# A chunked delta-rule recurrence: its output product in two PSUM banks, plain transposes of the keys, one prefix sum per pair of heads

## The chip, the cores and the metric

One NeuronCore of a Trainium2 chip runs the whole program in one launch. The metric is the device time of that launch in microseconds. Three runs of the kernel before are known, and one execution was profiled; every row below is from that one.

## The reference, cut to what matters

Two layers run over 1024 tokens of width 1024: a gated linear recurrence with convolution first, an RWKV-7 time mixer second, each followed by a SwiGLU and a gated projection. The change touches the RWKV-7 scan alone, which for each of 16 heads keeps a 64x64 state:

```
def step(S, inp):
    r_t, w_t, k_t, v_t, a_t, b_t = inp
    sa = jnp.einsum('bhvk,bhk->bhv', S, a_t)
    S = S * w_t[:, :, None, :] + sa[..., None] * b_t[:, :, None, :] + v_t[..., None] * k_t[:, :, None, :]
    y = jnp.einsum('bhvk,bhk->bhv', S, r_t)
    return S, y
```

The rest of the layer (projections, norms, SwiGLU, about 11,000 dense matmuls of 128x128 by 128x512) is the bulk of the arithmetic.

## The kernel before

Tokens are split into two halves of 512 (`t` = 0, 1), each half into eight chunks of 64. The scan is done chunk by chunk, for all 16 heads at once, two heads to a tile of 128 partitions (`HV` names the two halves E and O). It is cut into four streams, written as Python generators in `scan`:

- `stage1`, once per pair of heads and half, prepares: prefix sums of the log decay (`L`), the scaled keys `BK`, the products `sc` (masked into `ZL` and `AB`) and the transposed keys `bkt`, which go to DRAM as `bk`. The transposed keys are multiplied by the decay of the whole chunk, since the right operand of the product is `dg`, an identity whose rows POOL has scaled by `PC`.
- `inverse`, once per two pairs, inverts a triangular matrix per chunk and head in blocks (`w`, `n`, `u`, `w`, `v`).
- `stage2`, the recurrence, 16 steps in all (8 chunks, twice). Each step does three products into the one bank `zu`: z (from state `SV` and `ZL`), u (from `V` and z), and the state's increment (from `BKc` and `SU`); each waits for the copy of the one before it. DVE then adds the increment to `ss`, the state times the decay, worked out before. At the end of the step comes the output `y`: for each of 8 pairs and 2 heads one matmul over all 128 rows (state times `ZL`) and one over 64 rows (`SU` times `ZL`) that adds to it in the same 64x64 piece of the bank `y`.
- `norm2` normalizes the output of a half, two pairs at a time (`bsum`, `yv`), once all its steps are done.

The dense layers around it call `tick()` after every matmul. `tick` steps each stream whose wait has run out on a planner's clock (`self.clock`, advanced by an assumed time for each matmul) and, for streams that say so, once one or two PSUM banks of the ring `b` are taken to be free (`bank_free`, `BANKS`). PE's instructions stand in exactly this order: scan pieces between dense matmuls. `until` stops the dense work until a stream has reached a point. The scan's own PSUM is `zu`, `y` and `BANKS` banks `b`; the dense matmuls have three more (`mm`). The other engines' orders are the scheduler's: `ahead(n)` raises the priority of what stands under it.

Dense weights arrive as 128x512 pieces (`raw`, by SP's queue), are split by ACT (L239) and POOL (L240) into two parts `whl`, and are used by 12 matmuls each.

Of the kernel before, what the change touches and what calls it, by code (L numbers as in the profile page):

```python
# [8 lines left out]
F32 = mybir.dt.float32  # L9
F32R = mybir.dt.float32r  # L10
AF = mybir.ActivationFunctionType
ALU = mybir.AluOpType
# [3 lines left out]
TH = 512  # L16
# [8 lines left out]

BANKS = 3
PACE = ((3, 1200), (2.5, 200))
LEAD_O, LEAD_F, LEAD_E, LEAD_P = 2, 2, 1, 2  # L30
IN = 2
# [28 lines left out]
class Kern:  # L60
# [47 lines left out]
    def ahead(self, n):  # L108

        return self.tc.high_priority(n) if self.region else nullcontext()  # L110
# [811 lines left out]
    def scan_begin(self, sp, pp):  # L922
        nc, A = self.nc, self.A
        self.sp, self.spp = sp, pp
        self.zu = pp.tile([128, KD, 64], F32, name="zu")
        self.yp = pp.tile([128, KD, 64], F32, name="y")
        self.Pp = sp.tile([128, NC, 65], F32, name="Pp")
        nc.vector.memset(self.Pp[:, :, 0:1], 1.0)
        self.D16 = sp.tile([128, 32, 16], F32, name="D16")
        nc.vector.memset(self.D16, 0.0)  # L930
        self.O64 = sp.tile([128, 2 * NC, 64], F32, name="O64")
        nc.gpsimd.memset(self.O64, 0.0)

        self.zl_d = [self.dr.tile([128, NC, KD, 320], F32, name=f"zl{t}") for t in range(2)]
        self.bk_d = [self.dr.tile([128, NC, KD, 128], F32, name=f"bk{t}") for t in range(2)]
        self.inv_d = [self.dr.tile([128, NC, KD, 64], F32, name=f"inv{t}") for t in range(2)]
        self.y_d = [self.dr.tile([128, KD, TH], F32, name=f"y{t}") for t in range(2)]

    def scan(self):
# [45 lines left out]
        def c3(x):  # L985
            return x.rearrange("p (c s) -> p c s", s=64)
# [8 lines left out]
        def stage1():  # L995
            Pp = self.Pp

            def prep(t, j):
                at = ld("a", j, t)
                sw = ld("w", j, t)  # L1000
                kt = ld("k", j, t)
                L = tt("L")
                for c in range(0, TH, 64):
                    nc.vector.tensor_tensor_scan(
                        L[:, c : c + 64], self.ones[:, 0:64], sw[:, c : c + 64], 0.0, ALU.mult, ALU.add)
                nc.scalar.activation(Pp[:, :, 1:65], c3(L), AF.Exp, scale=-C0)
                nc.scalar.activation(L, L, AF.Exp, scale=C0)
                return at, kt, L, ld("q", j, t), sw

            nxt = None  # L1010
            for P, (t, g, jj) in enumerate(order):
# [17 lines left out]
                    PCs[t] = sp.tile([128, NC, KD], F32, tag="PC", name="PC", bufs=2)  # L1029
                PC = PCs[t][:, :, j]  # L1030
                nc.vector.tensor_copy(PC, Pp[:, :, 64])

                dg = sp.tile([128, NC, 64], F32, tag="dg", name="dg", bufs=1)
                nc.gpsimd.tensor_mul(dg, ident.unsqueeze(1).to_broadcast([128, NC, 64]), PC.unsqueeze(2).to_broadcast([128, NC, 64]))

                old = (P - 3) // 2
                yield 4000, False, (lambda: old < 0 or inv[old] >= 2)
# [49 lines left out]
                pss = [c3(big("bkt", e)) for e in (500, 900)]  # L1087
                for c in range(NC):
                    for hh, me, ot in HV:
                        self.mm(pss[hh][:, c, :], BK[me, c, :, :].rearrange("p i s -> p (i s)"), dg[me, c, :])  # L1090
                        self.clock -= 77
                evac()
                evac()
                with self.ahead(AHEAD_S1):
# [86 lines left out]
        def stage2():  # L1181
# [3 lines left out]
            def state():  # L1185
                return sp.tile([128, 2, KD, 64], F32, tag="SV", name="SV", bufs=2)
# [21 lines left out]
            for t in range(2):  # L1208
                yield 0, False, (lambda: inv[4 * t + 3] == 3 and s1[4 * t + 3] == 22 and all(have("v", j, t)() for j in range(KD)))
                PC = PCs[t]  # L1210
                nxt = load(t, 0, SV)
                yield C0LAT, False, None
                for c in range(NC):
                    ZL, V, SV = nxt
                    SU, BKc = load_u(t, c)
                    upd = not (t == 1 and c == NC - 1)
                    ps, yp = self.zu, self.yp
                    z = sp.tile([128, KD, 64], F32, tag="z", name="z", bufs=1)
                    at = self.clock
                    for j in range(KD):  # L1220
                        for hh, me, ot in HV:
                            self.mm(ps[me, j, :], ZL[:, j, hh * 128 : hh * 128 + 64], SV[:, hh, j, :])
                    self.clock = at + 650
                    with ahead():
                        nc.scalar.copy(z, ps)
                        if upd:
                            ss = sp.tile([128, KD, 64], F32, tag="ss", name="ss", bufs=1)
                            for hh, me, ot in HV:
                                nc.vector.tensor_mul(ss[me], SV[me, hh], PC[me, c, :].unsqueeze(2).to_broadcast([64, KD, 64]))
                            SVn = state()  # L1230
                        if c < NC - 1:
                            nxt = load(t, c + 1, SVn)
                    yield ZLAT, False, None
                    at = self.clock
                    for j in range(KD):
                        for hh, me, ot in HV:
                            self.mm(ps[me, j, :], V[me, j, :], z[me, j, :])
                    self.clock = at + 600
                    with ahead():
                        nc.scalar.copy(SU[E, 0], ps[E])  # L1240
                        nc.vector.tensor_copy(SU[O, 1], ps[O])
                    yield ULAT, False, None
                    at = self.clock
                    if upd:
                        for j in range(KD):
                            for hh, me, ot in HV:
                                self.mm(ps[me, j, :], BKc[:, j, hh * 64 : hh * 64 + 64], SU[:, hh, j, :])
                        with ahead():
                            for hh, me, ot in HV:
                                nc.vector.tensor_add(SVn[me, hh], ps[me], ss[me])  # L1250
                    for j in range(KD):
                        for hh, me, ot in HV:
                            self.mm(yp[me, j, :], SV[:, hh, j, :], ZL[:, j, hh * 128 + 64 : hh * 128 + 128], True, False)
                            self.mm(yp[me, j, :], SU[me, hh, j, :], ZL[me, j, 256:320], False, True)
                    self.clock = at + 2000
                    if c % 2 == 0:
                        ys = sp.tile([128, KD, 2, 64], F32, tag="yc", name="yc", bufs=1)
                    with ahead():
                        nc.scalar.copy(ys[:, :, c % 2, :], yp)
                    if c % 2:  # L1260
                        nc.sync.dma_start(self.y_d[t][:, :, c * 64 - 64 : c * 64 + 64], ys.rearrange("p j c k -> p j (c k)"))
                    if upd:
                        SV = SVn
                    s2[t] = c + 1
                    yield SLAT, False, None
# [223 lines left out]
```

## Time and profile before

| | us |
|---|---|
| median of 3 runs (lowest, highest) | 3225.04 (3216.24, 3226.09) |
| profiled execution, its own time | 3224.65 |
| its span, first to last instruction | 3222.9 |
| PE (matmul) busy | 3038.5, 94% |
| DVE, ACT, POOL busy | 50%, 42%, 40% |
| mean granted clock of TensorE | 0.950 of 2.4 GHz |

Busy shares are means over the whole span; which engine limits a stretch is read in the windows of that stretch. A matmul of plain fp32 leaves two records in the trace, so a block of 16 of them is a row of 32. The recurrence runs from about 1523 to 1766 us and from 2311 to 2535 us.

### The profile page before, as it was taken

The numbers are of one execution on the slowest core, as the hardware profiler recorded it, in microseconds if no ns is written. First come the engines' busy times: TensorE is split into PE (matmuls) and PEld (weight loads), VectorE is DVE, ScalarE is ACT, GpSimd is POOL, SyncE is SP. The second block draws the span as 40 slices with busy tenths as digits, with TensorE's granted clock in tenths as the row PEclk, the third lists the DMA queues.
The fourth block names the chain that finished last, engine by engine and source line by source line (L and its number), as shares of the span: only waits on it lengthen the run. The fifth ranks groups of instructions, "written<-read, shape, count | busy, mean of one in ns | idle before, by whom it ended". The sixth has DMA issues, their size and how long they took to land. (4 is left out here: it accounts for less than half of the span.)

```text
span 3222.9 us, 45692 instructions
## 1 busy us (share of the span) xinstructions
PE 3038.5 (94%) x17160; PEld 2386.2 (74%) x17160; DVE 1618.0 (50%) x2498; ACT 1359.2 (42%) x2213; POOL 1301.1 (40%) x1082
## 2 busy tenths in 40 slices
PE   5999999999999889999999878888999999999998
PEld 4777778887867667777777556667777777888886
DVE  8765751222572467773336556688322356312145
ACT  5574742323565334334344752333322345422244
POOL 5111144444554445444223354443322345544445
PEclk9999999999999989999888998889988899999999
DMA  3111133332336464444443676544444363333323
GB/s 126 59 43 45 51 98 95 95 95 92 119 118 211 155 207 159 156 146 135 151 155 107 221 231 187 174 139 155 134 135 153 105 220 104 105 95 95 95 84 106
DMA packets 269148, 415.20 MB, mean 129 GB/s; under 512 B 40704, under 2 KB 108032, under 8 KB 266880
## 3 DMA queue, kind: packets, MB, share of 16 engines
q1 hardware_dynamic: 268640, 411.93, 39.9%
q8 instruction: 135, 2.21, 0.3%
q14 instruction: 85, 0.70, 0.1%
q10 hardware_dynamic: 288, 0.37, 0.0%
HBM read 319.92 MB, written 92.27 MB: 128 GB/s over the span
## 5 line engine op out<-in xcount | busy, mean ns | idle before, releaser
L240 POOL TENSOR_TENSOR whl<-raw,whl 128x512 fp32r<-128x512 f32 (+2 forms) x818 | 1052.4, 1292 | 1511.6 <-ACT whl L239 1458.2
L239 ACT CAST whl<-raw 128x512 fp32r<-128x512 f32 (+2 forms) x818 | 482.6, 593 | 927.2 <-PE ops L116 249.4
L116 PE MATMUL pg<-xn,whl 128*128 128x512 f32 (+1 forms) x2184 | 524.5, 394 | 7.0 <-ACT xn L290 4.8
L116 PE MATMUL ops<-hid,whl 128*128 128x512 f32 x2112 | 513.1, 400 | 19.0 <-ACT hid L290 7.2
L116 PEld LDWEIGHTS ops<-hid,whl 128*128 128x128 f32 x2112 | 400.8, 192 | 119.6 <-DVE hid L291 14.3
L116 PEld LDWEIGHTS pg<-xn,whl 128*128 128x128 f32 x2184 | 408.1, 189 | 101.9 <-ACT xn L290 6.7
L116 PE MATMUL pu<-xn,whl 128*128 128x512 f32 x1584 | 384.3, 396 | 2.4 <-ACT xn L290 1.5
L116 PEld LDWEIGHTS pu<-xn,whl 128*128 128x128 f32 x1584 | 298.9, 190 | 70.1 <-DVE xn L291 2.1
L116 PE MATMUL pps<-mix,whl 128*128 128x512 f32 x1152 | 297.6, 412 | 15.2 <-ACT mix L290 4.6
L391 DVE TENSOR_TENSOR h<-h,ops 128x512 f32<-128x512 f32 x256 | 173.7, 685 | 265.2 <-PE ops L116 264.0
L556 DVE TENSOR_TENSOR sg<-sg,pu 128x512 f32<-128x512 f32 x88 | 60.3, 685 | 445.0 <-PE pu L116 444.6
L116 PEld LDWEIGHTS pps<-mix,whl 128*128 128x128 f32 x1152 | 220.5, 194 | 82.1 <-issue 11.4
L116 PE MATMUL pg<-raw,whl 128*128 128x512 f32 x720 | 195.2, 424 | 3.3 <-ACT whl L239 2.6
L116 PEld LDWEIGHTS pg<-raw,whl 128*128 128x128 f32 x720 | 145.9, 206 | 39.6 <-ACT whl L239 3.0
L242 POOL TENSOR_SCALAR whl<-raw 128x512 fp32r<-128x512 f32 (+2 forms) x84 | 59.7, 714 | 214.3 <-PE rps L116 74.0
L116 PE MATMUL pu<-raw,whl 128*128 128x512 f32 x528 | 142.0, 420 | 2.4 <-ACT whl L239 1.8
L116 PE MATMUL rps<-xn,whl 128*128 128x512 f32 x480 | 123.2, 404 | 15.4 <-ACT xn L290 9.5
L116 PEld LDWEIGHTS pu<-raw,whl 128*128 128x128 f32 x528 | 105.7, 203 | 28.4 <-ACT whl L239 2.2
L116 PEld LDWEIGHTS rps<-xn,whl 128*128 128x128 f32 x480 | 91.9, 193 | 41.6 <-issue 11.1
L116 PE MATMUL gps<-xn,whl 128*128 128x512 f32 x480 | 117.5, 399 | 0.0
L116 PE MATMUL ops<-m,whl 128*128 128x512 f32 x480 | 114.5, 396 | 0.8 <-ACT m L290 0.8
L291 DVE TENSOR_TENSOR hid<-sg,hid 128x512 fp32r<-128x512 f32 x88 | 86.3, 980 | 49.8 <-ACT hid L290 49.7
(276 smaller groups left out, 4022.1 us busy)
## 6 DMA issues: line engine op xcount, KB each, us to landing
raw<-in_ffn_in SPq DMA_DIRECT2D x352, 256.0 KB, 2.6
raw<-in_ffn_out SPq DMA_DIRECT2D x152, 256.0 KB, 2.6
raw<-in_rkv SPq DMA_DIRECT2D x96, 256.0 KB, 3.1
zl<-ZL SPq DMA_DIRECT2D x32, 640.0 KB, 3.9
ZC<-zl SPq DMA_DIRECT2D x16, 1280.0 KB, 5.7
raw<-in_ple_gate SPq DMA_DIRECT2D x64, 256.0 KB, 2.7
raw<-in_w_in SPq DMA_DIRECT2D x48, 256.0 KB, 2.8
h<-h SPq DMA_DIRECT2D x32, 256.0 KB, 3.3
```

What stands on the lines that cost most here:

```text
L116: self.nc.tensor.matmul(out, lhsT=lhsT, rhs=rhs, start=start, stop=stop)
L239: nc.scalar.copy(hl[:rows, 0, :w], raw[:rows, :w])
L240: nc.gpsimd.tensor_sub(hl[:rows, 1, :w], raw[:rows, :w], hl[:rows, 0, :w].bitcast(F32))
L242: nc.gpsimd.tensor_scalar(hl[:rows, 0, :w], raw[:rows, :w], 1.0, 0.0, ALU.mult, ALU.add)
L291: (nc.gpsimd if pool else nc.vector).tensor_sub(lo, src, hi.bitcast(F32))
L391: nc.vector.tensor_add(hs, hs, ps)
L556: nc.vector.tensor_mul(sg, sg, pu)
```

## The change

1. The output goes to two banks, `yp[0]` and `yp[1]`. All 16 matmuls over 128 rows (state times `ZL`) are done right behind z into the first, all 16 over 64 rows (`SU` times `ZL`) behind the state's increment into the second. ACT copies the first bank, and DVE adds the second to the copy, which it did not do before.
2. The second bank is taken from the ring `b`: `BANKS` is 2. So two free banks now means all of them.
3. `bkt` is a plain transpose of `BK` with the identity, an instruction of another kind. The multiplication that made `dg` on POOL is gone. The state is therefore updated as (state + increment) times decay: an add and a multiplication per half, both behind the increment, where the multiplication used to stand ahead of it.
4. One prefix sum over 512 elements replaces eight over 64. Its factor `run` is 1, and 0 at each chunk's start.
5. The planner's clock is charged 1300, 600 and 1300 ns in a step instead of 650, 600 and 2000, and the next chunk's loads are no longer raised in priority.

```diff
-BANKS = 3
+BANKS = 2
...
-        self.yp = pp.tile([128, KD, 64], F32, name="y")
+        self.yp = [pp.tile([128, KD, 64], F32, name=f"y{i}") for i in range(2)]
...
+            run = sp.tile([128, TH], F32, name="run")
+            nc.gpsimd.memset(run, 1.0)
+            nc.gpsimd.memset(c3(run)[:, :, 0:1], 0.0)
...
-                for c in range(0, TH, 64):
-                    nc.vector.tensor_tensor_scan(
-                        L[:, c : c + 64], self.ones[:, 0:64], sw[:, c : c + 64], 0.0, ALU.mult, ALU.add)
+                nc.vector.tensor_tensor_scan(L, run, sw, 0.0, ALU.mult, ALU.add)
...
-                dg = sp.tile([128, NC, 64], F32, tag="dg", name="dg", bufs=1)
-                nc.gpsimd.tensor_mul(dg, ident.unsqueeze(1).to_broadcast([128, NC, 64]), PC.unsqueeze(2).to_broadcast([128, NC, 64]))
...
-                        self.mm(pss[hh][:, c, :], BK[me, c, :, :].rearrange("p i s -> p (i s)"), dg[me, c, :])
-                        self.clock -= 77
+                        nc.tensor.transpose(pss[hh][:, c, :], BK[me, c, :, :].rearrange("p i s -> p (i s)"), ident[me])
+                        self.clock += 30
...
-                    self.clock = at + 650
+                    for j in range(KD):
+                        for hh, me, ot in HV:
+                            self.mm(yp[0][me, j, :], SV[:, hh, j, :], ZL[:, j, hh * 128 + 64 : hh * 128 + 128])
+                    self.clock = at + 1300
                     with ahead():
                         nc.scalar.copy(z, ps)
-                        if upd:
-                            ss = sp.tile([128, KD, 64], F32, tag="ss", name="ss", bufs=1)
-                            for hh, me, ot in HV:
-                                nc.vector.tensor_mul(ss[me], SV[me, hh], PC[me, c, :].unsqueeze(2).to_broadcast([64, KD, 64]))
-                            SVn = state()
-                        if c < NC - 1:
-                            nxt = load(t, c + 1, SVn)
+                    if upd:
+                        SVn = state()
+                    if c < NC - 1:
+                        nxt = load(t, c + 1, SVn)
...
                         with ahead():
+
+                            w = sp.tile([128, KD, 64], F32, tag="w", name="w", bufs=1)
                             for hh, me, ot in HV:
-                                nc.vector.tensor_add(SVn[me, hh], ps[me], ss[me])
+                                nc.vector.tensor_add(w[me], ps[me], SV[me, hh])
+                                nc.vector.tensor_mul(SVn[me, hh], w[me], PC[me, c, :].unsqueeze(2).to_broadcast([64, KD, 64]))
                     for j in range(KD):
                         for hh, me, ot in HV:
-                            self.mm(yp[me, j, :], SV[:, hh, j, :], ZL[:, j, hh * 128 + 64 : hh * 128 + 128], True, False)
-                            self.mm(yp[me, j, :], SU[me, hh, j, :], ZL[me, j, 256:320], False, True)
-                    self.clock = at + 2000
+                            self.mm(yp[1][me, j, :], SU[me, hh, j, :], ZL[me, j, 256:320])
+                    self.clock = at + 1300
...
-                        nc.scalar.copy(ys[:, :, c % 2, :], yp)
+                        nc.scalar.copy(ys[:, :, c % 2, :], yp[0])
+                        nc.vector.tensor_add(ys[:, :, c % 2, :], ys[:, :, c % 2, :], yp[1])
```

Three places of the order, each with its rows before and after. The first is PE in the first step of the recurrence (`pu`, `pg`, `ops`, `pq` and `nps` are dense, a number at the end is a count). Before:

```order
L116 MATMUL zu<-SV,ZC 64x64 x16
L116 MATMUL pu<-xn,whl 128x512 x11
L116 MATMUL pg<-xn,whl 128x512 x2
L116 MATMUL zu<-z,VC 64x64 x16
L116 MATMUL pg<-xn,whl 128x512 x13
L116 MATMUL zu<-SU,BC 64x64 x16
L116 MATMUL y<-ZC,SV 64x64
L116 MATMUL y<-ZC,SU 64x64
...
```

The last two rows go on by turns until each stands 16 times. The same place of the changed kernel:

```order
L116 MATMUL zu<-SV,ZC 64x64 x16
L116 MATMUL y_8222<-ZC,SV 64x64 x16
L116 MATMUL ops<-hid,whl 128x512 x13
L116 MATMUL zu<-z,VC 64x64 x16
L116 MATMUL ops<-hid,whl 128x512 x3
L116 MATMUL pg<-raw,whl 128x512 x10
L116 MATMUL zu<-SU,BC 64x64 x16
L116 MATMUL y_8223<-ZC,SU 64x64 x16
```

The 32 matmuls by turns became two blocks of 16 of one kind, and the first of them moved up behind z. The recurrence also starts 139 dense matmuls later in the program than before (position 5758 of the dense matmuls instead of 5619).

The second place is PE at the end of the scan, where its last two output groups stand (`bsum`, `yv`). Before:

```order
L116 MATMUL bsum<-b,cst 128x512 x2
L116 MATMUL ops<-hid,whl 128x512 x29
L116 MATMUL yv<-v,cst 128x512 x2
L116 MATMUL ops<-hid,whl 128x512 x48
L116 MATMUL pu<-raw,whl 128x512 x3
```

The changed kernel there:

```order
L116 MATMUL bsum<-b,cst 128x512 x2
L116 MATMUL ops<-hid,whl 128x512 x29
L116 MATMUL yv<-v,cst 128x512 x2
L116 MATMUL ops<-hid,whl 128x512 x36
L116 MATMUL bsum<-b,cst 128x512 x2
L116 MATMUL yv<-v,cst 128x512 x2
L116 MATMUL pu<-raw,whl 128x512 x24
```

The last group moved behind the last dense matmul that the planner has for it, and nothing dense stands between its two products now. The 48 dense matmuls that stood behind the group's end are gone from there.

The third place is DVE at the first step's state update (`SU` is the copy of u, `h`, `raw`, `acc` and `ph` belong to dense layers). Before:

```order
L1241 COPY SU<-zu 64x512
L1250 TENSOR_TENSOR SV<-zu,ss 64x512 x2
L1229 TENSOR_TENSOR ss<-SV,PC 64x512 x2
```

The changed kernel:

```order
L1240 COPY SU<-zu 64x512
L391 TENSOR_TENSOR h_86<-h_86,ops 128x512
L343 SCALAR_TENSOR_TENSOR raw<-h_86,vec,raw 128x512
L302 TENSOR_TENSOR acc<-acc,sq 128x512
L1251 TENSOR_TENSOR w<-zu,SV 64x512 x2
L1252 TENSOR_TENSOR SV<-w,PC 64x512 x2
L1261 TENSOR_TENSOR yc<-yc,y_8223 128x8x64
```

Two instructions stood between the increment and the new state's use, four do now, and the addition of the second output bank follows them.

## Rows read from the trace of the kernel before

**Rows 1.** The page: busy us of an engine, share of the span, instructions.

```profile
PE 3038.5 (94%) x17160; PEld 2386.2 (74%) x17160; DVE 1618.0 (50%) x2498; ACT 1359.2 (42%) x2213; POOL 1301.1 (40%) x1082
```

**Rows 2.** Windows: length, busy us per engine (instructions), granted clock, DMA.

```profile
core 0: us, PE busy (x) PEld busy (x) DVE busy (x) ACT busy (x) POOL busy (x), PEclk, DMA share, GB/s
1080.00:1520.00 440.00, 406.47 (x3186) 323.63 (x3185) 295.99 (x561) 168.78 (x291) 200.41 (x156) 0.95 0.52 165
1520.00:1766.00 246.00, 245.05 (x1830) 188.24 (x1829) 112.62 (x150) 100.14 (x167) 70.05 (x55) 0.88 0.42 135
2270.00:2535.00 265.00, 265.00 (x2147) 205.99 (x2148) 69.29 (x95) 70.88 (x115) 67.47 (x51) 0.86 0.39 126
```

**Rows 3.** Timeline of PE, one step: start, length, instruction and its count.

```profile
1523.50 1.15 PE L116 MATMUL zu<-SV,ZC 128*64 128x64 f32 x32
...
1524.58 2.79 PE L116 MATMUL pu<-xn,whl 128*128 128x512 f32 x11
...
1527.75 1.15 PE L116 MATMUL zu<-z,VC 64*64 64x64 f32 x32
...
1532.98 0.28 PE L116 MATMUL y<-ZC,SV 128*64 128x64 f32 x2
...
1539.59 0.47 PE L116 MATMUL y<-ZC,SU 64*64 64x64 f32 x2
...
1542.41 3.88 PE L116 MATMUL pg<-xn,whl 128*128 128x512 f32 x9
...
1546.13 5.64 PE L116 MATMUL pu<-xn,whl 128*128 128x512 f32 x24
...
1553.96 1.15 PE L116 MATMUL zu<-SV,ZC 128*64 128x64 f32 x32
```

**Rows 4.** Windows of the instructions on tile y alone, same columns as rows 2.

```profile
1520.00:1766.00 246.00, 76.97 (x512) 55.76 (x512) 2.04 (x3) 4.69 (x8) 5.17 (x3) 0.88 0.42 135
2270.00:2535.00 265.00, 79.93 (x512) 57.62 (x512) 0.00 (x0) 4.69 (x8) 0.00 (x0) 0.86 0.39 126
```

**Rows 5.** Timeline of PE around one bkt block.

```profile
1190.02 2.00 PE L116 MATMUL bkt<-dg,BK 64*128 64x64 f32 x32
1191.95 1.89 PE L116 MATMUL pu<-xn,whl 128*128 128x512 f32 x7
```

**Rows 6.** Instructions on tile bkt: ns min/median/max, first and last start.

```profile
L116 PEld LDWEIGHTS bkt<-dg,BK x512: 182/188/334, 1143.8 to 2249.6; 64*128 64x128 f32 x171
L116 PE MATMUL bkt<-dg,BK x512: 272/272/473, 1143.8 to 2249.6; 64*128 64x64 f32 x171
```

**Rows 7.** DVE by form: busy us, mean ns, idle before and releaser.

```profile
L1004 DVE TENSOR_TENSOR_SCAN L<-ones,w 128x64 f32<-128x64 f32 x128 | 31.6, 299 | 20.2 <-DMA w<-w 13.2 <-DMA b<-r 6.2 <-DVE h L391 0.8
...
L1229 DVE TENSOR_TENSOR ss<-SV,PC 64x512 f32<-64x512 f32 x30 | 25.1, 836 | 0.6
...
L1250 DVE TENSOR_TENSOR SV<-zu,ss 64x512 f32<-64x512 f32 x30 | 20.6, 687 | 14.9 <-PE zu L116 14.0 <-DMA raw<-in_ffn_out 0.6
...
L482 DVE TENSOR_TENSOR_SCAN hr<-a,hr,b 128x512 f32<-128x512 f32 x8 | 10.3, 1284 | 0.3
```

**Rows 8.** Timeline of all engines, end of the recurrence's last output groups.

```profile
2601.83 1.88 PE L116 MATMUL yv<-v,cst 128*128 128x512 f32 x4
...
2612.35 0.32 SPq L1302 DMA_DIRECT2D o<-ys  x1
...
2618.85 1.13 PE L116 MATMUL bsum<-b,cst 128*128 128x512 f32 x2 [0.53 <-DMA b<-b]
...
2621.38 0.63 ACT L1286 ACTIVATE v<-ys 128x512 f32<-128x512 f32 x1
...
2627.72 11.49 PE L116 MATMUL ops<-hid,whl 128*128 128x512 f32 x48
...
2642.48 0.73 PE L116 MATMUL pg<-raw,whl 128*128 128x512 f32 x2 [2.59 <-ACT whl L239]
```

**Rows 9.** Waits of PE over the span: us in total, times, longest.

```profile
PE sc L116 <- DVE ZL L1072: 16.8, 4, 6.1
```

## The prediction, made before the changed kernel ran

> **What bounds the kernel now.** I read the page first, then windows by stage, then one step of the recurrence instruction by instruction. The page says that PE is busy for 94% of the span and no other engine for more than half [rows 1]. That is a mean over stages, so the stretches of the scan come next [rows 2]. In the preparing stage (1080 to 1520 us) PE idles for 33.5 us and DVE is at 67%: PE sometimes waits there. In the two stretches that hold the recurrence PE idles for 1 us of 246 and for none of 265, while DVE is at 46% and 26%. There PE alone is the bound, and what is taken off PE comes off the end. The same rows show a granted clock of 0.88 and 0.86, against 0.95 in the stage before: part of the time PE runs at the lower level, 1.2 instead of 2.4 GHz.
>
> One step shows why [rows 3]. The block for z, 32 records, starts at 1523.50, and the dense matmul behind it at 1524.58: 1.08 us, or 34 ns a record. The block for u, over 64 rows, has the same length as z's, 1.15 us with the overlap at its end. The output, 64 records of the same two kinds that differ only in standing by turns, runs from 1532.98 to 1542.41: 9.43 us, 147 ns a record. Two records take 0.28 us at its start and 0.47 us near its end, and the dense matmuls behind it are slow too: nine of them from 1542.41 to 1546.13, 3.72 us. Elsewhere 48 take 11.49 us, 0.239 us each [rows 8], so nine should take 2.15. The clock fell inside the output block and came back some 3 us after it.
>
> **The change, part by part.** *The output.* It costs 76.97 + 79.93 = 156.9 us of PE [rows 4]. In its place stand two blocks of one kind in each of 16 steps. The first has z's rows, operands and output size, the second u's; z's block is 1.08 us [rows 3], so 16 x 2 x 1.08 = 34.6 us. Gain **122 us**. No wait hides it, as PE does not idle in these stretches. If the new blocks do not run as z's do, the gain is smaller; that is rival C.
>
> *The clock.* Behind the output of the step shown, 3.72 - 2.15 = 1.6 us are lost to the lower level. Over the first stretch: 246.0 - 1.0 idle - 77.0 of output - 24 blocks x 1.08 leaves 142.1 us for 1830 - 512 - 768 = 550 other matmuls [rows 2, 4], 0.258 each where 0.239 is the full pace: 10.5 us, 1.3 a step. I take 1.5 x 16 = **24 us** gained, since what remains are blocks of 2.2 us at most, and the 11 dense matmuls behind z's block of 1.08 us still run at 0.25 us each [rows 3]. Bounds 0 and 26.
>
> *The transposes.* A block of `bkt` takes 1.93 us [rows 5], 16 of them 31 us. No transposing instruction is in this trace, so its price is bounded. From below: if each leaves one record where it leaves two now, half, 15 us gained. From above: nothing overlaps, and each of the 256 takes a weight load and a matmul one after the other, 188 + 272 ns [rows 6], 118 us, 87 lost. The nearest row is `bkt` itself, with the same operands and shapes and the same turns between halves, so I stay between no change and half: **8 us** gained. The Trainium skill, "TensorE: Matmul & The Clock Gate", Part 4, puts a transpose at about 275 ns within a kernel and says that the clock gate does not count it as work; by that 256 of them would be 70 us, the sum 3125 us instead of 3078. No run here shows it yet.
>
> *DVE and POOL in the preparing stage.* Eight prefix sums at 0.299 us become one; the trace has a sum of 512 elements at 1.28 [rows 7]. That is 16 x 1.1 = 18 us less for DVE, and POOL loses 16 multiplications. The addition of the second output bank is new: one 512-element instruction with a PSUM operand, as L1250 at 0.687 us [rows 7], 11 us in all, in stretches where DVE is half idle. All this lies beside PE. It can shorten PE's waits for DVE, of which the products `sc` have 16.8 us [rows 9].
>
> *Two banks instead of three.* Now the second product `sc` of a pair needs both banks of the first back, where it needed one. The order puts 29 dense matmuls between them instead of 22, 1.7 us more, about what DVE needs to empty the second bank (1024 elements in three instructions, by the 0.687 us for 512 in [rows 7]). I set this against the relief of DVE and take **0** for both, with bounds from 10 us gained to 17 lost (the 16.8 us of waits doubled).
>
> *The state's update.* Behind the increment stand an add and a multiplication for each half, 2 x (0.687 + 0.836) = 3.0 us [rows 7], where two adds stood. From the increment's end to the next z there are 21.0 us now (1532.98 to 1553.96 [rows 3]); without the long output, and with the dense matmuls at full pace, 21.0 - 9.4 + 1.1 - 1.6 = 11. So 8 us of cover stay: **0**. Next in line is the load of the next chunk, which is no longer raised in priority. It has the whole step, some 20 us instead of 30, and stands among SP's weight loads; rival B prices it.
>
> *The end of the scan.* The recurrence starts 139 dense matmuls later in the program and gives most but not all of it back, so the last output group has no dense work between its two products or ahead of the first. Today a group's second `bsum` comes 17.0 us behind the `yv` of the group before (2601.83 to 2618.85 [rows 8]), as the group before must first store its results (until 2612.35) and hand over its buffers. In the new order PE has 1.9 + 36 x 0.239 = 10.5 us of work in that time and waits for 6.5. From that `bsum` to the squares that `yv` needs are 3.2 us (to 2621.38 + 0.62), bare now. Today PE waits 2.6 us for weights at this place (2642.48); behind the new `yv` stand 48 matmuls whose weights SP loads ahead of that group. So 6.5 + 3.2 - 2.6 = **7 us** lost, with bounds 0 and 15.
>
> The sum goes from the profiled execution's own 3224.65 us (span 3222.9), which is 0.4 under the median of the three runs, so nothing is corrected: 3224.65 - 122 - 24 - 8 + 0 + 0 + 7 = 3077.65, **3078 us**. With all favourable bounds (26, 15, 10, 0) it is 3052. With the unfavourable ones of transposes that change nothing, banks and end (0, +17, +15) it is 3111. That is the forecast's own range.
>
> **The rivals.** *A, the transposes are dear.* They come without overlap. At the row-made bound of 0.46 us each the time is 3078 + 8 + 87 = 3173 us. For it: no row shows them. Against: loads and matmuls of the two halves overlap in `bkt` today, 32 pairs in 1.93 us though one pair alone would be 0.46. Chance 7%. The page named above has this rule, at a lower price.
>
> *B, a new wait in the shorter step.* PE reaches the next z 10 us sooner, and the next chunk's loads, the weights or DVE do not. At 2 to 5 us in each of 16 steps that is 3110 to 3158 us. For it: the same transfers in less time bring the DMA share of 0.42 to 0.42 x 246 / 174 = 0.59 (246 - 77 + 17 - 12 = 174 us). Against: in the preparing stage DMA is at 0.52 with 165 GB/s, and PE is busy for 92% beside a DVE at 67% [rows 2]. Chance 10%.
>
> *C, the change does not do what it says.* The price lies in these matmuls themselves, not in the turns, and only half of it goes: 78 us instead of 35 for the output and half of the clock's loss: 3078 + 43 + 12 = 3133 us. Against: z and u, the same two kinds, run at 34 ns a record a few us earlier. Chance 4%.
>
> *D, slower.* The new state or the next chunk's `ZL` comes so late that z must wait as long as the output takes today. The gain outside the end is 146 us, 9.1 a step; so it decides from 20 us behind the increment, where 3.0 us of DVE work are queued. At 21 us behind it the time is 3078 + 16 x 10 = 3238 us. DVE at 46% [rows 2] speaks against it. Chance 2%.
>
> **How the numbers follow.** The forecast has 77%. Its own range is 3052 to 3111. The range for 8 in 10 goes from 3050 to 3125: that takes in the mild end of B and a rival A in which a good third of the loss comes (3078 + 8 + 36 = 3122), and leaves out the rest of A and B, and C. What this kernel's measurement can tell from no change is about 0.3%, 10 us. All cases but D, and a B three times as dear, are faster by more than that: faster 96%, the same 2%, slower 2%.
>
> **What would show it.** Right: the output as two rows of 32 records of about 1.15 us in each step, a granted clock of 0.95 or more in the recurrence's stretches, dense matmuls behind each block at 0.24 us, 16 blocks `bkt` under 2 us, one prefix sum of 1.3 us per pair, and PE waiting some 10 us in all at the last `bsum` and `yv`. Wrong: PE idle before `zu` or for `whl` in every step (B, D), a block `bkt` of 4 us or more with slow dense matmuls behind it (A), or records of the output well above 34 ns (C).

## The result and the profile after

The changed kernel takes 3062.11 us (median of four runs, 3060.83 to 3070.75) where the kernel before takes 3224.53 on the same chip: ratio 0.9507, 95% interval 0.9483 to 0.9531, 162 us less. The profiled execution took 3070.75 us, the longest of the four; a second one, of 3058.4 us, comes with the first experiment.

The page of the changed kernel (busy us, share, instructions; against [rows 1]): PE's share is as before, with 166 us less in it.

```profile
PE 2872.9 (94%) x16904; PEld 2259.7 (74%) x16904; DVE 1613.8 (53%) x2402; ACT 1354.8 (44%) x2213; POOL 1282.4 (42%) x1068
```

Windows of the changed kernel, columns as in [rows 2], cut at the scan's own milestones, so that versions can be compared: from 1080 us to the first `zu`, the first recurrence, to the first `ops<-on`, to the second recurrence, that recurrence, from its last `zu` to 40 us behind the last `yv`, and the rest.

```profile
1080.00:1548.00 468.00, 433.10 (x3214) 341.37 (x3214) 303.54 (x522) 186.36 (x322) 206.04 (x162) 0.95 0.52 162
1548.00:1717.00 169.00, 161.29 (x1700) 127.15 (x1700) 116.58 (x152) 97.14 (x168) 68.14 (x51) 0.98 0.62 195
1717.00:1922.00 205.00, 178.03 (x807) 128.64 (x807) 117.13 (x169) 117.20 (x202) 87.62 (x68) 0.93 0.70 224
1922.00:2243.00 321.00, 279.01 (x2488) 220.05 (x2489) 231.53 (x418) 123.33 (x214) 133.77 (x104) 0.93 0.51 158
2243.00:2381.00 138.00, 138.00 (x1597) 113.03 (x1593) 58.88 (x84) 46.74 (x78) 46.51 (x35) 1.00 0.63 201
2381.00:2515.00 134.00, 120.19 (x518) 89.49 (x517) 64.72 (x84) 56.66 (x97) 55.97 (x47) 0.95 0.57 184
2515.00:3069.00 554.00, 535.67 (x2338) 435.81 (x2338) 197.83 (x243) 207.91 (x352) 272.20 (x209) 0.99 0.31 96
```

The same stretches of the kernel before, cut in the same way:

```profile
1080.00:1524.00 444.00, 410.47 (x3217) 326.77 (x3217) 296.68 (x562) 171.72 (x296) 201.70 (x157) 0.95 0.52 164
1524.00:1748.00 224.00, 223.05 (x1691) 172.20 (x1687) 101.30 (x137) 88.99 (x149) 65.81 (x53) 0.89 0.44 143
1748.00:2007.00 259.00, 219.91 (x987) 159.14 (x983) 156.45 (x244) 144.46 (x249) 110.57 (x82) 0.91 0.63 203
2007.00:2311.00 304.00, 269.94 (x2468) 216.94 (x2468) 210.68 (x412) 110.69 (x192) 123.34 (x99) 0.90 0.48 151
2311.00:2515.00 204.00, 204.00 (x1572) 157.29 (x1571) 54.47 (x75) 51.86 (x84) 47.27 (x36) 0.86 0.41 135
2515.00:2666.00 151.00, 147.20 (x637) 113.21 (x637) 73.02 (x89) 62.08 (x105) 65.55 (x53) 0.94 0.53 175
```

The lengths differ also because dense work has moved from one stretch to another, so the idle time (length minus PE's busy time) and the granted clock are what to read. In the recurrences the clock is 0.98 and 1.00 instead of 0.89 and 0.86. Idle are 34.9, 7.7, 27.0, 42.0, 0, 13.8 and 18.3 us, where before they were 33.5, 0.9, 39.1, 34.1, 0, 3.8 and, in the rest, 19.2. Over the span idle time grew by 12 us, 184.4 to 196.1. At the end of the scan it grew by 10; 6.8 more in the first recurrence and 7.9 more ahead of the second stand against 12.1 less behind the first.

The same windows view for the instructions on the output tile alone, against [rows 4]: 36.85 us of PE where there were 156.9.

```profile
1520.00:1740.00 220.00, 18.84 (x512) 17.02 (x512) 8.23 (x12) 4.64 (x8) 8.57 (x4) 0.98 0.58 186
2200.00:2420.00 220.00, 18.01 (x512) 16.24 (x512) 5.49 (x8) 4.70 (x8) 0.00 (x0) 1.00 0.53 168
```

The timeline of PE (start, length, instruction and count, in brackets the idle time before it), one step as in [rows 3], a block of transposes as in [rows 5], the output projection of the first half (`on` is the normalized output that it reads), and the end of the scan as in [rows 8]:

```profile
1147.42 0.71 PE L1089 MATMUL bkt<-cst,BK 64*128 64x64 f32 x16
...
1547.90 1.15 PE L116 MATMUL zu<-SV,ZC 128*64 128x64 f32 x32
1548.88 1.10 PE L116 MATMUL y<-ZC,SV 128*64 128x64 f32 x32
1549.92 3.24 PE L116 MATMUL ops<-hid,whl 128*128 128x512 f32 x13
...
1557.34 1.15 PE L116 MATMUL zu<-SU,BC 128*64 128x64 f32 x32
1558.42 1.15 PE L116 MATMUL y<-ZC,SU 64*64 64x64 f32 x32
...
1779.12 2.07 PE L116 MATMUL bsum<-b,cst 128*128 128x512 f32 x2 [8.26 <-DMA b<-b]
...
1943.64 6.53 PE L116 MATMUL ops<-on,whl 128*128 128x512 f32 x17 [15.08 <-ACT on L290]
...
2425.93 1.13 PE L116 MATMUL bsum<-b,cst 128*128 128x512 f32 x2 [1.74 <-DMA b<-b]
...
2447.51 0.51 PE L116 MATMUL ops<-hid,whl 128*128 128x512 f32 x1 [1.46 <-ACT hid L290]
...
2472.98 1.10 PE L116 MATMUL bsum<-b,cst 128*128 128x512 f32 x2 [2.51 <-DMA b<-b]
2474.96 3.78 PE L116 MATMUL yv<-v,cst 128*128 128x512 f32 x4 [0.88 <-ACT v L1288]
2479.52 7.97 PE L116 MATMUL pu<-raw,whl 128*128 128x512 f32 x24 [0.78 <-ACT v L1297]
2490.18 0.70 PE L116 MATMUL pg<-raw,whl 128*128 128x512 f32 x2 [2.69 <-issue]
```

The two output blocks are 1.04 and 1.08 us to the next instruction's start. The 13 dense matmuls behind the first take 3.17 us, 0.244 each, where 0.239 is the full pace: the clock no longer falls. A block of 16 transposes takes 0.64 us to the next start, 40 ns each.

Waits of PE over the span (total, times, longest). The products `sc` wait as long as in [rows 9]; what is new stands behind the first recurrence, at the end of the scan, and before the transposes (`Wa` is a block of `inverse`).

```profile
PE sc L116 <- DVE ZL L1071: 16.4, 9, 4.0
PE ops L116 <- ACT on L290: 15.1, 1, 15.1
PE bsum L116 <- DMA b<-b: 14.7, 4, 8.3
PE bkt L1089 <- DVE Wa L1149: 12.3, 4, 4.1
```

In the kernel before the second and third of these were 4.6 and 0.5 us, and `bkt` waited 4.6 us, for `ZL`. In the second profiled execution of the changed kernel the wait for `Wa` is 6.7 us, so its size varies between executions.

So the profiled execution's gain of 153.9 us of span is 165.6 us less of PE's busy time and 11.7 us more of idle time. Of the 165.6, 156.9 - 36.85 = 120.0 are the output and 16 x (1.93 - 0.64) = 20.6 the transposes; the 25.0 that are left are the same other work, done faster. By the starts in the two traces the dense matmuls of the two recurrences lost some 24 us to a pace slower than 0.239 us before, and some 2 us after, so that gain lies where the clock rose.

### The profile page after: what moved, and what is told of

It reads as the page before. It is cut to its first block, busy times and chain, and to the rows that moved or that the text cites. A ratio compares the mean times of both kernels' runs of the same rounds, so it can differ in the third digit from the quotient of the medians.

```text
span 3069.0 us, 45111 instructions
## 1 busy us (share of the span) xinstructions
PE 2872.9 (94%) x16904; PEld 2259.7 (74%) x16904; DVE 1613.8 (53%) x2402; ACT 1354.8 (44%) x2213; POOL 1282.4 (42%) x1068
## 4 chain that ended last, share of the span: by engine, by line
PE 36%; DVE 10%; DMA 6%; issue 4%; POOL 3%; ACT 2%; SPq 1%; DVEq 0%; POOLq 0%; ACTq 0%
PE pg L116 11%; PE ops L116 9%; PE pu L116 8%; PE pps L116 2%; DMA zl<-ZL 2%; POOL whl L240 2%; PE zu L116 1%; DMA raw<-in_ffn_in 1%; PE pq L116 1%; PE y L116 1%; DVE X L1131 1%; DVE W L1128 1%; DVE ZL L1071 1%; ACT whl L239 1%; DVE h L391 1%
## 5 line engine op out<-in xcount | busy, mean ns | idle before, releaser
L116 PE MATMUL ops<-hid,whl 128*128 128x512 f32 x2112 | 504.8, 395 | 10.3 <-ACT hid L290 4.6
L116 PEld LDWEIGHTS ops<-hid,whl 128*128 128x128 f32 x2112 | 393.4, 188 | 105.8 <-DVE hid L291 10.3
L116 PE MATMUL pps<-mix,whl 128*128 128x512 f32 x1152 | 300.7, 415 | 14.4 <-ACT mix L290 4.6
L116 PE MATMUL pg<-raw,whl 128*128 128x512 f32 x720 | 181.6, 401 | 7.1 <-POOL whl L240 3.2
L116 PEld LDWEIGHTS pg<-raw,whl 128*128 128x128 f32 x720 | 135.2, 191 | 40.5 <-POOL whl L240 4.9
L116 PEld LDWEIGHTS rps<-xn,whl 128*128 128x128 f32 x480 | 91.9, 193 | 42.2 <-issue 11.7
```

Source lines behind the costliest of these rows:

```text
L116: self.nc.tensor.matmul(out, lhsT=lhsT, rhs=rhs, start=start, stop=stop)
```

## The experiments

Every kernel is the changed one but for its edit, unless it says otherwise. The theory is the prediction's: the time lay in the turns between the two kinds of rows, most of it as PE time and the rest as a lower clock. The rival mechanisms for the output are that a matmul adding into what was just written is slow, or that two parts in one bank are; for the rest, that the preparing stage or the scan's end decides. Times are medians, with the lowest and highest run in brackets and then the ratio to the kernel before with its 95% interval. Kernels run on different occasions are compared by that ratio; most intervals reach some 0.0015, 5 us, to either side, so that a difference of two ratios is uncertain by about 7 us.

**The changed kernel again**, no edit.

> The changed kernel once more, beside the next three, so that they have it on the same chip. Theory: the runs of it so far lie at 3061 to 3071 us, and this one lies there too. In its profile the two blocks of the output are 1.1 us each, and the last output group makes PE wait about 15 to 20 us at the end of the scan, as in the first profile, if that loss belongs to the order of the instructions; a rival has it as chance of that one execution (its 3071 us are 9 us above the other runs), and then the waits at the end are under 10 us here.

3066.25 us (3058.4 to 3069.3), ratio 0.9508 (0.9492 to 0.9524). `ops` waits 14.9 us for `on` and `bsum` 14.7 for its load again, and 16.1 us are idle at the end of the scan: these losses belong to the program's order and are no chance.

**The output by turns again, but into two banks and without adding.** The first part's loop goes back behind the increment:

```diff
-                    for j in range(KD):
-                        for hh, me, ot in HV:
-                            self.mm(yp[0][me, j, :], SV[:, hh, j, :], ZL[:, j, hh * 128 + 64 : hh * 128 + 128])
...
                         for hh, me, ot in HV:
+                            self.mm(yp[0][me, j, :], SV[:, hh, j, :], ZL[:, j, hh * 128 + 64 : hh * 128 + 128])
                             self.mm(yp[1][me, j, :], SU[me, hh, j, :], ZL[me, j, 256:320])
```

> The changed kernel with the 32 output matmuls of a step by turns again at the end of the step, but still into two banks, with no adding on top of what was just written. Theory (the turns cost): the output takes about 9.4 us a step again, the granted clock in the recurrence falls under 0.9, and the time is 3062 + 130 to 146 = 3192 to 3208 us. Rival (the price is that the second product adds to the piece that the first has just written, in one bank): the output stays near 2.2 us a step and the time near 3062 us. If both count, something between.

3209.8 us (3206.85 to 3213.03), ratio 0.9950 (0.9935 to 0.9965): 143.6 us more than the changed kernel beside it, near the upper end of the theory's range. Its windows, output tile alone:

```profile
1520.00:1800.00 280.00, 77.52 (x512) 56.11 (x512) 8.15 (x12) 4.68 (x8) 6.98 (x4) 0.88 0.45 143
2240.00:2560.00 320.00, 77.40 (x512) 55.99 (x512) 5.48 (x8) 4.68 (x8) 0.00 (x0) 0.90 0.42 136
```

154.9 us of PE, as in [rows 4], with nothing added and each part in a bank of its own. The price is the turns'; both rivals fall. Of the 143.6 us, 154.9 - 36.9 = 118 are the output itself and 25.5 the clock's and whatever else follows from it.

**One bank and adding, but in blocks.** One matmul of zeros opens the bank in each step, and both blocks add into it:

```diff
-        self.yp = [pp.tile([128, KD, 64], F32, name=f"y{i}") for i in range(2)]
+        self.yp = pp.tile([128, KD, 64], F32, name="y")
...
+                    nc.tensor.matmul(yp.rearrange("p j k -> p (j k)"), lhsT=self.zz, rhs=self.run, start=True, stop=False)
...
-                            self.mm(yp[1][me, j, :], SU[me, hh, j, :], ZL[me, j, 256:320])
+                            self.mm(yp[me, j, :], SU[me, hh, j, :], ZL[me, j, 256:320], False, j == KD - 1)
```

> The changed kernel with both parts of the output in one bank again, still as two blocks of one kind: a matmul by zeros opens the whole bank, the 128-row block adds to it behind z, the 64-row block adds to it at the end, ACT copies once and DVE adds nothing. BANKS stays 2, so the order is the same but for the 16 zero matmuls of one pass over 512 columns (0.21 to 0.4 us each, 4 to 6 us in all). Theory (only the turns cost, neither the one bank nor the adding on top): blocks of 1.1 us, time 3066 + 4 to 6, less what DVE's missing additions give, 3062 to 3072 us. Rival (adding into the bank costs as well): blocks well above 1.1 us and 3090 us or more.

3079.02 us (3075.43 to 3080.25), ratio 0.9553 (0.9537 to 0.9569), 15 us over the changed kernel by the ratios. By groups (busy us, mean ns | idle before) its blocks are as short as those into two banks:

```profile
L116 PE MATMUL y<-ZC,SU 64*64 64x64 f32 x512 | 19.2, 227 | 0.0
L116 PE MATMUL y<-ZC,SV 128*64 128x64 f32 x512 | 18.4, 225 | 0.0
L1225 PE MATMUL y<-run,zz 128*128 128x512 f32 x16 | 8.0, 503 | 0.0
```

So in blocks adding costs next to nothing either. The time missed all the same: it lies above the theory's range and below the rival's. The 16 opening matmuls explain some 7 to 8 of the 15 us, and the waits of `zu` another 3 to 4 (8.1 us, in the changed kernel 4.1 and 4.7); the rest was not traced.

**The same with the third bank back for the scan** (`BANKS = 3`).

> The same kernel with the bank that this frees given back to the ring: BANKS = 3. The recurrence then starts where it did in the kernel before, 139 dense matmuls earlier, and its last group has dense work behind it again. Theory (the third bank's loss cost the changed kernel its waits for Wa before the transposes, 7 to 12 us, the 15 us before the w_o projection of the first half and the 17 to 19 us at the end): 3066 + 5 - 25 to 35 = 3036 to 3046 us, with these waits under 5 us each. Rival (the two banks cost nothing that reaches the end, the losses come from the faster recurrence itself): 3062 us or more, as in the run with two banks.

3075.19 us (3075.06 to 3079.08), ratio 0.9542 (0.9528 to 0.9557). The theory missed. Windows of this kernel, from 1080 us to the first `zu` and at the end of the scan:

```profile
1080.00:1526.00 446.00, 402.99 (x3092) 318.52 (x3092) 296.18 (x507) 170.69 (x296) 191.82 (x150) 0.95 0.53 164
2378.00:2518.00 140.00, 136.60 (x614) 105.50 (x614) 74.72 (x93) 63.91 (x109) 68.24 (x56) 0.99 0.60 190
```

The end of the scan in its sister with two banks:

```profile
2385.00:2519.00 134.00, 118.09 (x517) 88.17 (x515) 64.79 (x83) 56.54 (x98) 56.51 (x47) 0.96 0.57 183
```

At the end 3.4 us are idle at a clock of 0.99, where its sister with two banks has 15.9 of 134 at 0.96, and the waits for `on` and for `bsum`'s loads fall to 5.2 and 3.6 us. But in the preparing stage 43.0 us of 446 are idle instead of 34.0 of 463 (over the span `n` waits 11.7 us for `Wa`, which suggests that the planner now sets these products closer together than DVE follows). Over the span the third bank still saves 9.4 us of idle time, 191.7 against 201.1, but PE is busy for 9.0 us more, and the granted clock of the four runs is 0.968 to 0.969 instead of 0.970 to 0.971. So here the third bank gave back 3.5 us by the ratios, which is no more than the noise; why PE is slower with it stays open.

**The kernel before with two banks for the scan** (`BANKS = 2` in the old kernel, nothing else).

> The kernel before with BANKS = 2 and nothing else (one PSUM bank lies idle). Theory (the smaller ring delays the recurrence and makes waits): 20 to 35 us slower, 3246 to 3260 us, with PE waiting at the end of the scan and before the w_o projection of the first half. Rival (the ring's size is free, as my prediction had it at 0 with bounds of -10 and +17): 3216 to 3232 us.

3239.3 us (3236.47 to 3245.65), ratio 1.0051 (1.0034 to 1.0069): 14.3 us lost, between the theory's range and the rival's. Windows, the same two places:

```profile
1080.00:1568.00 488.00, 453.74 (x3347) 360.62 (x3346) 310.89 (x579) 186.88 (x320) 216.26 (x169) 0.94 0.50 156
2537.00:2688.00 151.00, 136.62 (x552) 100.75 (x550) 64.14 (x83) 57.23 (x98) 56.75 (x47) 0.89 0.51 164
```

The preparing stage is no worse in idle time (34.3 us, before 33.5), while 14.4 us are idle at the end instead of 3.8, and the clock there is 0.89 instead of 0.94. Over the span idle time is nearly the same (185.9 to before's 184.4, since the projections wait less), and PE is busy for 19.4 us more with the same instructions: mean granted clock 0.947 instead of 0.950. So in this execution the loss shows as slower work and not as more waiting. But it is the longest of the four; the other three, 3236 to 3241 us, have clocks of 0.950 to 0.952, where the runs of the kernel before beside them have 0.951 to 0.953. How much of the 14.3 us is the clock's is therefore not shown. PE waits 15.1 us for `bsum`'s loads, as in the changed kernel, but not for `on`.

**The keys by matmul** with the identity, not by a transpose:

```diff
-                        nc.tensor.transpose(pss[hh][:, c, :], BK[me, c, :, :].rearrange("p i s -> p (i s)"), ident[me])
+                        nc.tensor.matmul(pss[hh][:, c, :], lhsT=BK[me, c, :, :].rearrange("p i s -> p (i s)"), rhs=ident[me], start=True, stop=True)
```

> The changed kernel with a plain matmul by the identity in place of the transpose of the keys; same operands, same order. Theory (the transposes are cheaper on PE and that reaches the end): a block bkt is 1.9 us instead of 0.64, so 16 x 1.3 = 20 us more, 3082 us. Rival (in the preparing stage PE waits for DVE anyway, and what a block gives is lost in the next wait): under 8 us more, 3062 to 3070 us. Third, by my prediction's term of 8 us: 3070.

3082.16 us (3080.39 to 3086.23), ratio 0.9556 (0.9542 to 0.9570), 15.9 us more than the changed kernel beside it, as the theory said. A block takes 1.93 to 1.94 us to the next start, as in [rows 5]: 16 x (1.93 - 0.64) = 20.6 us of PE, of which 15.9 show in the medians (the two profiled executions lie 23 apart). The group leaves two records for each matmul again; its row, and below it the changed kernel's:

```profile
L1089 PE MATMUL bkt<-cst,BK 64*128 64x64 f32 x512 | 34.2, 279 | 6.6 <-DVE Wa L1149 6.6
L1089 PE MATMUL bkt<-cst,BK 64*128 64x64 f32 x256 | 13.6, 243 | 12.3 <-DVE Wa L1149 12.3
```

**Eight prefix sums again** in place of one:

```diff
-                nc.vector.tensor_tensor_scan(L, run, sw, 0.0, ALU.mult, ALU.add)
+                for c in range(0, TH, 64):
+                    nc.vector.tensor_tensor_scan(
+                        L[:, c : c + 64], self.ones[:, 0:64], sw[:, c : c + 64], 0.0, ALU.mult, ALU.add)
```

> The changed kernel with its prefix sums cut back into eight scans of 64 columns, 128 of them in all where the changed kernel has 16; nothing else differs. One scan of 64 took 299 ns before, one of 512 takes 1224 ns in the changed kernel, so that VectorE gets back about 16 times 8 x 299 - 1224 = 1168 ns, 18.7 us. Theory of the prediction (VectorE is not what the preparing stage waits for): within 10 us of the changed kernel, 3062 to 3076. Rival (VectorE's chain sets the preparing stage, and the freed time is what pays there): 15 to 20 us more, 3080 to 3087, with longer waits of TensorE on VectorE's Wa and scores before 1520 us.

3081.81 us (3069.47 to 3083.76), ratio 0.9554 (0.9541 to 0.9567), 14.8 us over the changed kernel by the ratios. The theory missed, and the rival is nearer: by the medians DVE's relief pays, by 8 to 21 us with the intervals taken together. The group of prefix sums on DVE, in this kernel and in the changed one:

```profile
L1008 DVE TENSOR_TENSOR_SCAN L<-ones,w 128x64 f32<-128x64 f32 x128 | 36.9, 338 | 14.2 <-DMA b<-r 8.7 <-DMA w<-w 5.5
...
L1007 DVE TENSOR_TENSOR_SCAN L<-run,w 128x512 f32<-128x512 f32 x16 | 22.7, 1416 | 11.5 <-DMA b<-r 6.4 <-DMA w<-w 5.1
```

The relief is 14 us of DVE's time, and 9 against the kernel before (31.6 us in [rows 7]), not the 18.7 of the expectation, which took the mean of the short sums and the median of the long one. The timeline of the profiled execution (3069.47 us, the shortest of the five) shows two long waits in the preparing stage, and below them the second place in the changed kernel's first profiled execution:

```profile
1407.59 4.79 PE L116 MATMUL pu<-xn,whl 128*128 128x512 f32 x14 [5.26 <-DVE sg L555]
...
1438.06 1.11 PE L1091 MATMUL bkt<-cst,BK 64*128 64x64 f32 x15 [4.29 <-DVE Wa L1151]
...
1434.48 1.11 PE L1089 MATMUL bkt<-cst,BK 64*128 64x64 f32 x15 [4.12 <-DVE Wa L1149]
```

The first wait, of a dense matmul for DVE (`sg` is a dense layer's gate), is 1.2 to 1.3 us and for weights in both profiled executions of the changed kernel. The second is 4.12 us in one of them and 1.37 in the other, so it is no sign of the prefix sums. From 1080 us to the first `zu` 37.9 us are idle, against 34.9 and 30.1; over the span 203.7, against 196.1 and 191.4. That the sums' length is worth some 15 us rests on the times alone; the trace shows 8 to 12 us more of idle time and one wait that may carry it, and the slower runs were not profiled.

**A shorter planned pause behind a step** (`SLAT` 2000 for 3000), in both halves:

> The changed kernel with the planner's pause behind each step of the recurrence cut from 3000 to 2000 ns (before pacing), so that a step takes some 13 dense matmuls less and the recurrence and the output groups behind it end about 100 dense matmuls earlier. Theory (the loss at the end of the scan comes from the last group standing behind the last dense matmul): the 15 to 20 us at the end go, 3062 - 15 = 3047 us. Rival (the shorter step makes z wait for the new state or for its loads): PE idles before zu in most steps, and the time is 3062 us or more.

3067.41 us (3063.34 to 3068.95), ratio 0.9506 (0.9492 to 0.9521): no change. The theory was half right: at the end of the scan 6.4 us are idle of 141 at a clock of 0.98, instead of 13.8 of 134 at 0.95, but the first recurrence and the stretch behind it have 10.9 and 33.5 idle instead of 7.7 and 27.0.

**The shorter pause in the second half alone:**

```diff
-                    yield SLAT, False, None
+                    yield SLAT - 1000 * t, False, None
```

> The changed kernel with the planner's pause cut from 3000 to 2000 ns in the second half's steps alone. In the run with both halves cut, the end gave back 17 us and the stretch of the first half's last steps and the projections behind them lost some 22 us against the same kernel with the full pause. Theory (the end's loss is the late last group; the other loss is a matter of where the first half's steps fall): the time is 3066 - 15 = 3048 to 3054 us, PE waits little at the last bsum and yv. Rival (the second half's steps lose in waits before zu what the end gives): 3060 us or more.

3050.0 us (3048.04 to 3056.04), ratio 0.9465 (0.9449 to 0.9480): 14 us less than the changed kernel, as the theory said. The end of the scan, as a window and as a timeline:

```profile
2352.00:2495.00 143.00, 136.34 (x608) 104.20 (x607) 71.78 (x94) 61.26 (x105) 63.99 (x53) 0.99 0.58 181
```

```profile
2446.61 1.88 PE L116 MATMUL bsum<-b,cst 128*128 128x512 f32 x4
2447.92 7.18 PE L116 MATMUL ops<-hid,whl 128*128 128x512 f32 x29
2454.94 1.88 PE L116 MATMUL yv<-v,cst 128*128 128x512 f32 x4
2456.26 7.63 PE L116 MATMUL ops<-hid,whl 128*128 128x512 f32 x31
2463.73 5.60 PE L116 MATMUL pu<-raw,whl 128*128 128x512 f32 x24
2470.97 0.71 PE L116 MATMUL pg<-raw,whl 128*128 128x512 f32 x2 [1.65 <-issue]
```

Dense matmuls stand between the last group's products again, and no wait for `bsum`'s load is left there: 6.7 us are idle of 143 at a clock of 0.99, and the first half is as in the changed kernel (7.3 and 27.6). But over the span 192.5 us are idle, no less than the 191.4 of the changed kernel's second profiled execution: what the end gives in idle time is lost again in small amounts elsewhere, and the gain shows as 9 us less of PE's busy time. The granted clock is 0.972 to 0.976 in the four runs, against 0.968 to 0.972 in the eight of the changed kernel. This version is faster than both kernels.

**A still shorter one** (`SLAT - 2000 * t`):

> The changed kernel with the planned pause behind a step of the recurrence cut from 3000 to 1000 in the second half of the sequence, and left at 3000 in the first (2000 in the second gave 3050). Theory: the second recurrence ends late by its planned pauses and the work kept back for them runs out before the end; 2000 took most of that wait away, so 1000 gives little more, or gives some back, because the steps then come closer than the data they wait for (loads of the next step's operands): 3045 to 3058. Rival: the end is still late at 2000, and 1000 gives another 8 to 15 us: 3035 to 3042.

3050.08 us (3048.47 to 3053.99), ratio 0.9461 (0.9448 to 0.9474): no more to be had there, as the theory said.

## Why the prediction was right, and by how much it was off

It gave 3078 us, and 3062 was measured, in the forecast's own range.

*The output*, 122 us: 156.9 - 36.85 = 120 measured. Blocks of one kind run as z's and u's do; rival C falls. The mechanism is shown: by turns in two banks the price is back, in blocks in one bank it is not.

*The clock*, 24 us: 25.5 by the kernel with the turns, 25.0 by the busy time of the two profiled executions, and a granted clock of 0.98 and 1.00 in the recurrences, where by the starts in the traces the dense matmuls gained some 22 us. Size and place are as forecast.

*The transposes*, 8 us: mis-sized. They are worth 15.9 us by the medians, a little over the favourable bound of 15, and 20.6 by the blocks. The prediction stayed between "no change" and "half the records" because the turns between the halves remain. A block went not to half of its 1.93 us but to a third, 0.64: half the records, and each 40 ns instead of 60. Rival A falls. The Trainium skill ("TensorE: Matmul & The Clock Gate", Part 4) puts a transpose at about 275 ns within a kernel, for 128x128 in bf16; taken as the time from one to the next, that would be, as an estimate, 4.4 us a block. The trace has 0.64: the record of one transpose is 223 ns long by the median, not far from that figure, but the records overlap, and the 40 ns between starts decide.

*DVE's relief and two banks*, 0 for both: the sum came out by luck, as two effects that the forecast did not see cancel. "All this lies beside PE" failed: by the times the one long prefix sum is worth some 15 us, about the 14 that it takes off DVE, though the traces do not show the whole way to PE. And two banks cost the old kernel 14.3 us, not at the second product `sc` (its waits there are 17.9 us, before 16.8), but with 10.6 us more of idle time at the end of the scan and with slower work. In the changed kernel with its output in one bank, the third bank gave back only 3.5 us, within the noise, so what two banks cost there is not settled.

*The state's update*, 0: the waits of `zu` are 3.9 us for `SU`, and none for the new state. It was not tried by itself. Rivals B and D, a wait in every step, did not come, though the DMA share rose from 0.42 in [rows 4] to 0.58 in the same window of the changed kernel, near the 0.59 that rival B had worked out.

*The end of the scan*, 7 us: 10 measured (idle 3.8 to 13.8 us), within the bounds, but only in part by the mechanism forecast. The last groups do stand bare, yet the waits at the last `bsum` and `yv` are 2.5 and 0.9 us where the forecast's sign was some 10: that `bsum` comes 13.4 us behind the `yv` of the group before, not 17.0. The wait of 2.6 us behind them, which the forecast took off the sum, is still there (2.7 us, with no releaser in the profile; 5.2 us for weights in the second execution), and 3.2 us stand at an earlier group's `bsum` and an earlier `ops`. That these errors nearly cancel is luck. The old kernel with two banks idles the same 10.6 us more there, and with the third bank back in the one-bank kernel 3.4 us are left, so this is a part of what two banks do and no term beside it. The pause's runs bear out that lateness is the cause: with the second half's steps planned closer the waits at the last group go, and the time falls by 14 us, though the profile shows that gain more as faster work than as less waiting.

Parts measured one at a time add up to the whole: -143.6 (turns, clock included) - 15.9 (transposes) - 14.8 (prefix sums) + 14.3 (two banks) = -160.0 us, against -159.6 measured beside the first of these runs. This is a check and no proof. Each part is uncertain by several us, and the price of two banks was taken in the old kernel; with the 3.5 us of the one-bank kernel the sum would be -170.8. The state's update, the planner's charges and the loads' lower priority were not tried by themselves. The forecast's 147 us were 8 too few for the transposes by the medians, and held 7 us of loss for the end beside an allowance for the two banks that already covered it; these two make up the 15 us to the 162 measured, and the rest of the agreement is in part the luck named above.

What stays open: the forecast had no term for the waits behind the first recurrence, and PE waits 8.3 us for the load of the first half's `bsum` and some 15 us for `on` at the first half's output projection in the changed kernel and in most versions of it. The wait for `on` is missing in the old kernel with two banks and in the kernel with the keys by matmul; no run was aimed at what decides that.

## What to carry to other kernels

Look at the order of matmuls of different row counts before their number: the same 1,024 records took 157 us by turns and 37 us in blocks of one kind, and the lower clock behind the turns cost another 25. An engine at 67% of a stage may still set it: price its relief by a run, not by its share. Where planned times set the order, look behind every stage that a change moves, since the work that covered a wait may have run out; here one pause in one half gave 14 us.

## What the runs showed of the hardware that was not expected

- Turns between matmuls over 128 and over 64 rows cost 147 to 153 ns a record, against 34 to 36 in blocks of one kind, adding in one bank or not adding in two. Turns between the upper and the lower 64 rows alone do not: the transposes make them at 40 ns and `zu` from `z` at 34 ns.
- At the end of the scan less waiting and a higher granted clock come together: 13.8 us idle at 0.95 in the changed kernel, 6.7 at 0.99 with the shorter pause. Elsewhere they do not: ahead of the second recurrence the changed kernel idles 42.0 us at 0.93 and the kernel before 34.1 at 0.90. So no run shows that a wait by itself costs clock.
- A transpose of f32 leaves one record where the matmul that does the same leaves two (256 and 512), with 13.6 and 34.2 us in them.
- One prefix sum over 512 elements takes 1.42 us by the mean (1.22 by the median), where eight over 64 take 8 x 0.299 = 2.39 by the mean [rows 7]. The short ones overlap, so that all sums together keep DVE busy for 22.7 us instead of 31.6. A multiplier of zero at each chunk's first element restarts it.
